# One fused Hyena and SwiGLU layer: the first joint reordered, late down-projection loads on GpSimd's queue, one operand of the last pair written down earlier

## The chip, the cores and the metric

The kernel runs on one core of one Trainium2 chip, as one program. The metric is device time in microseconds of one execution; it is given as the median of the runs, with the lowest and the highest beside it. The core has five engines with a queue each: TensorE (PE in the profile, with PEld for its weight loads), VectorE (DVE), ScalarE (ACT), GpSimd (POOL) and SyncE (SP). DMA transfers are issued here by SP (queue q1) and by POOL (queue q0), and some by ACT. Each engine carries out its queue in order; semaphores tie the queues together.

## The reference, cut to what matters

One layer on 1024 tokens of width 1024, in float32:

```python
h = rmsnorm(x, norm_mix)
z = short_conv(h @ w_in + b_in)           # 3 x 1024 columns
x0, x1, v = split(z);  s = v * x1
g = hyena_filter(...)                     # implicit long filter, 2L taps
y = irfft(rfft(s, 2L) * rfft(g, 2L))[:L]
x = x + ((y + s * skip) * x0) @ w_out + b_out
x = x + (silu(u @ w_gate) * (u @ w_up)) @ w_down,   u = rmsnorm(x, norm_ffn)
out = rmsnorm(x, norm_final)              # FFN hidden width 2816
```

## The kernel before

Every product is carried out in split float32: an operand is stored as a high part (a rounded copy, made by ACT) and a low part (what is left, a subtraction), and a product is three matmuls (`TERMS`): high by high, high by low, low by high. The low part is made in one of two ways. `split` (L128 to L130) has ACT copy the high part and DVE subtract. `low_dma` (L148 to L150) has ACT write minus the high part, and a POOL DMA that adds the source onto it in flight.

**Stages.** The input projection and the Hyena mixer run block by block up to about 410 us. The output projection follows: half 0 of its columns (`out_part`, over k = 0 to 7 of the contraction and four pairs of token blocks m), with the last block's inverse transform (`inverse_mm`) between k = 6 of pair 1 and k = 6 of pair 2; then half 1, a loop over the eight token blocks in the order `seq` = 0, 4, 1, 5, 2, 3, 6, 7 (L1310 on). This loop is the first part of the joint. Step n of it has 24 products for block j, then `turn` (eight transposes) of the block before, `x1_half` (DVE adds the residual, ACT squares, SP stores it to DRAM), `normed` (the RMS norm of the row block, in place, on DVE with a square root on ACT), and `post`, which makes the operands of the FFN from the transposed block.

**The FFN** multiplies two by two blocks in Winograd's form with seven products instead of eight. Its right operands are B11, B21, B22 and four combinations T1 to T4 of the transposed, normed blocks: `top_left` (L1091) makes the blocks of m = 0 to 3 that go into B11 and B21, with their low parts by `low_dma` for m < 3 and by DVE for m = 3; `top_sums`, with `Right`, makes T1 to T4 and B22 of blocks 4 to 7. Its left operands come from weights loaded as `wgr` and `wur`: a `Unit` is one pair of 128 hidden columns of gate or up, with a11 to a22 and four sums s[0] to s[3] (`sums`, `sum3`, `sum4`). The products of a unit are a (a11 by B11), b (a12 by B21), f, g, e (s[1], s[2], s[0] by T2, T3, T1), d (a22 by T4) and c (s[3] by B22). PSUM tiles `ab` and `dc` hold two halves each: pa and pb, pd and pc. `p1` is product a, `p1_out` copies pa away, `p2` adds product b. `w_op` (L1191) makes a left operand's two parts in one of five buffers, `OPS`, which rotate in the order in which the calls stand.

From L1306 on PE, DVE and ACT are in an order written out by hand (`manual_schedule`): first the loop, and from L1347 the rest of the joint, in which the last two blocks (6 and 7) are turned and combined while the first two units (`ug` for gate, `uu_` for up, pair 0) begin. Four weight operands there, `pre` and `pq`, are made ahead by `early_op` (L1302), which is a split by `low_dma`: `pre` holds a11 of both units, `pq` a12. POOL and SP are placed by the planner in this stage. The planner orders what isn't written by hand by a modelled timeline.

Pairs 1 to 9 (`pair`) follow, placed by the planner with SP by hand; pair 10 is `last_pair`, with PE by hand. Its results go to DRAM (`HD`), and the down projection reads them back: `product2` for p1, p5, p6, p3, p7, p2, p4, six batches each. `operands` (L1544) loads a batch's left operand on POOL (`hr`, four buffers), splits it, and splits the weights from `wds`, the down weights, which SP has loaded as quads B11, B12, B22, B21 of eleven blocks, with quarters of the residual (`load_y1`) between them. `less` forms differences of quads in place on DVE (L1614).

Of the kernel before, what the change touches and what calls it, by code (L numbers as in the profile page):

```python
# [102 lines left out]
def hyena_ffn_kernel(ctx: ExitStack, tc: tile.TileContext, a: dict, out: bass.AP):  # L103
# [904 lines left out]
    out_part(0, (6,))  # L1008
    out_part(1, (6,), (0, 1))
    inverse_mm(b)  # L1010
    out_part(1, (6,), (2,))
# [79 lines left out]
    def top_left(m, pt):  # L1091
        ms = cols_of(m)
        S.copy(u2[0][0][:, :, ms], pt)
        xt = x1[m].rearrange("p (k m) -> p k m", k=NB)
        S.copy(xt, pt)
        if m < 3:
            low_dma(u2[0][0][:, :, ms], u2[1][0][:, :, ms], xt)
            return lambda: None
        return lambda: V.tensor_tensor(
            u2[1][0][:, :, ms], pt, u2[0][0][:, :, ms].bitcast(F32), ALU.subtract  # L1100
        )
# [95 lines left out]
    class Unit:  # L1197
# [57 lines left out]
        def sums(u, eng):  # L1255
            eng.tensor_tensor(u.s[0], u.a21, u.a22, ALU.add)
            eng.tensor_tensor(u.s[1], u.s[0], u.a11, ALU.subtract)
# [40 lines left out]
    def post_late():  # L1298
        while late:
            late.pop(0)()  # L1300
# [5 lines left out]
    with tc.manual_schedule(  # L1306
# [3 lines left out]
        for n, j in enumerate(seq):  # L1310
            if n % 4 < 2:
                pts[n % 2] = mm_psum(f"po1{n}")
            hf = n // 2 % 2
            o = pts[n % 2][:, hf * 512 : (hf + 1) * 512]
            for k in range(NB):
                out_mm(o, 1, j, k)
            if n == 1:
                t_op("T1", "ab_g", ("gg0",))
                t_op("T2", "cr", ("fwd01",))
                t_op("T3", "whl1", ("hs", "wt"))  # L1320
            if 1 <= n <= 6:
                turn(seq[n - 1])
            if n == 7:
                turn(6)
                pq = slot("ss", "pq", (2, 2, 4, P), F32R)
                early_op(pq[:, 0], ug.a12)
            x1_half(j, 1, o)
            if n == 6:
                early_op(pre[:, 1], uu_.a11)
            if n < 7:  # L1330
                post_late()
                normed(j)
            if 1 <= n <= 6:
                post(seq[n - 1])
            if n == 3:
                ug = Unit(0, wg, "wg")
            if n == 4:
                uu_ = Unit(0, wu, "wu")
                pre = slot("whl0", "pre", (2, 2, 4, P), F32R)
            if n == 5:  # L1340
                early_op(pre[:, 0], ug.a11)
            if n == 6:
                post_late()
                ug.s_tag = "ab_d"
                ug.split_sum_tiles()
                ug.sums(V)
        ug.begin(True)  # L1347
        uu_.begin(True)
        r6 = Right(2, turns[6])
        r6.sums12()  # L1350
        norm_begin(7)
        r6.sum3()
        r6.high("T2")
        r6.b22_high()
        norm_end(7)
        ug.p1(pre[:, 0])
        r6.high("T3")
        r6.low("T3", None)
        early_op(pq[:, 1], uu_.a12)
        r6.low("T2", V)  # L1360
        r6.b22_low()
        ug.p1_out()
        ug.early = {"f": w_op("wg0f", ug.s[1])}
        uu_.p1(pre[:, 1])
        turn(7)
        r6.sum4()
        r6.high("T1")
        r6.low("T1", None)
        uu_.p1_out()
        r7 = Right(3, turns[7])  # L1370
        r7.sums12()
        r7.sum3()
        ug.p2(pq[:, 0])
        uu_.p2(pq[:, 1], (0, 1))
        r6.t4_high()
        r6.t4_low(None)
        r7.part("T2", V)
        r7.part("T3", V)
        ug.sum3()
        ug.early["g"] = w_op("wg0g", ug.s[2])  # L1380
# [3 lines left out]
        ug.product(ug.pb, "f", None, "T2", True, ug.early["f"])  # L1384
        V.tensor_tensor(ug.uu[:, 1], ug.uu[:, 0], ug.pb, ALU.add)
        r7.t4_high()
        r7.t4_low(None)
        r7.b22_high()
# [4 lines left out]
        ug.product(ug.pd, "e", None, "T1", True, ug.early["e"])  # L1393
        ug.sum4()
        g0 = slot("inv", "g0", (4, 512))
        ug.early["d"] = w_op("wg0d", ug.a22)
        uu_.sum_tiles()
        uu_.sums(V)
        uu_.early["f"] = w_op("wu0f", uu_.s[1])
        ug.end_products(g0[:, 1:4])  # L1400
        uu_.sum3()
        uu_.early["g"] = w_op("wu0g", uu_.s[2])
        S.activation(g0[:, 0], ug.pa, AF.Silu)
        ug.end_sums(g0[:, 1:4])
        uu_.sum4()
        uu_.product(uu_.pb, "f", None, "T2", True, uu_.early["f"])
        V.tensor_tensor(uu_.uu[:, 1], uu_.uu[:, 0], uu_.pb, ALU.add)
# [4 lines left out]
    def pair(i, ug=None, uu_=None):  # L1412
        early = ug is not None
        g = g0 if early else slot("inv", f"g{i}", (4, 512))
        if not early:
# [4 lines left out]
            ug.sums(V)  # L1420
# [5 lines left out]
        if not early:  # L1426
# [4 lines left out]
            uu_.sums(V)  # L1431
# [25 lines left out]
    def last_pair(i):  # L1457
# [6 lines left out]
        ug.sums(V)  # L1464
        uu.p1()
        uu.p1_out()
        ug.product(ug.pb, "f", ug.s[1], "T2", True)
# [7 lines left out]
        uu.sums(V)  # L1475
# [29 lines left out]
    def load_quad(x, i):  # L1505
        f, d = divmod(x, 2)
        load(wds[i][:, x], wd[i * 256 + f * P : i * 256 + (f + 1) * P, d * 512 : (d + 1) * 512])
# [4 lines left out]
    def load_y1(r, c):  # L1512
        for q in range(4):
            j, cs = 4 * r + q, slice(c * 512, (c + 1) * 512)
            load(y1[j][:, cs], X1D[j][:, cs])
# [28 lines left out]
    def operands(nm, hx, wsrc, i, n):  # L1544
# [4 lines left out]
        store(hr[:, 0:n], HD[hx][:, i : i + n, :])  # L1549
        ho = hi_lo(SETS[c][0], f"ho{nm}{i}")  # L1550
# [98 lines left out]

    bx = four(mm_psum, "bx")  # L1650
# [9 lines left out]
    V.tensor_scalar(gfin, gfin, 2.0, None, ALU.mult)  # L1660
    for i in range(NP):
        load_quad(B21, i)
    load_y1(1, 0)
# [37 lines left out]
```

## Time and profile before

| | us |
|---|---|
| median of 3 runs | 1176.32 (1175.88 to 1178.87) |
| profiled execution, time | 1177.2 |
| profiled execution, span | 1175.4 |
| PE busy | 1151.6 (98%) |
| DVE busy | 870.8 (74%) |
| ACT busy | 522.3 (44%) |
| POOL busy | 155.1 (13%) |

The profile is of one execution. The span runs from its first to its last instruction. A busy time is the sum over an engine's instructions; PE's includes work done at a lower granted clock. "L1237" is line 1237 of the kernel; an arrow reads "written tile <- read tiles", with buffer numbers left out; a bracket in a timeline row gives the engine's idle time just before it and what ended that. Times in timeline rows are microseconds from the span's start, first the start, then the length of the row, which can hold several instructions (x4).

### The profile page before, as it was taken

The page shows a single profiled execution, that of the slowest core. Times are in us where ns is not written, and L with a number is a line of the kernel's source. Part 1 is how long each engine was busy: PE and PEld are TensorE (multiplying, and loading weights), DVE is VectorE, ACT ScalarE, POOL GpSimd, SP SyncE. Part 2 cuts the span into 40 slices and gives each one's busy share as a digit, 9 for nine tenths or more (in the row PEclk, how much of TensorE's full clock was granted, in tenths as well). Part 3 has the DMA queues.
Part 4 walks back from the last instruction along what each step waited for, and adds up shares of the span by engine and source line. Part 5 has one row for each costly group of instructions (what it writes and reads, how often), then busy time and mean ns, then how long its engine had stood idle before and what let it go on. Part 6 is the DMA issues. An engine that isn't in the chain of part 4 may idle for free.

```text
span 1175.4 us, 15154 instructions
## 1 busy us (share of the span) xinstructions
PE 1151.6 (98%) x5714; PEld 970.0 (83%) x5714; DVE 870.8 (74%) x1389; ACT 522.3 (44%) x829; POOL 155.1 (13%) x218
## 2 busy tenths in 40 slices
PE   8999999999999999988999999999999999999997
PEld 6889898898988888876888888888888788788886
DVE  7688989889898895477756676666566567955675
ACT  8563553545446474365333233323333243334445
POOL 0010211112011141052001110111011110110100
PEclk9999999999999999999999999999999999999999
DMA  7456778776674799576223332324133269833323
GB/s 240 145 120 144 141 163 170 159 166 155 129 161 100 195 245 298 148 138 105 96 101 120 105 115 69 130 90 135 56 124 108 75 231 374 297 117 96 99 81 144
DMA packets 105818, 172.95 MB, mean 147 GB/s; under 512 B 7181, under 2 KB 65933, under 8 KB 105616
## 3 DMA queue, kind: packets, MB, share of 16 engines
q0 software_dynamic: 30080, 81.02, 30.5%
q1 hardware_dynamic: 75517, 90.70, 23.3%
q8 instruction: 45, 0.74, 0.2%
q10 hardware_dynamic: 146, 0.27, 0.1%
q14 instruction: 30, 0.24, 0.1%
HBM read 101.96 MB, written 40.11 MB: 121 GB/s over the span
## 4 chain that ended last, share of the span: by engine, by line
PE 85%; DVE 7%; DMA 6%; ACT 1%; issue 1%; POOL 0%; DVEq 0%; POOLq 0%; ACTq 0%; SPq 0%
PE z L140 20%; PE bx L1560 8%; PE po L914 3%; PE bz L1560 3%; PE by L1560 3%; PE pg L541 2%; PE pp L614 2%; PE pg L540 2%; DMA wd<-in_ffn_w_down_dram 2%; DMA xd<-x 1%; DMA wohl<-wo 1%; PE py L653 1%; PE py L654 1%; PE z L366 1%; PE z L693 1%; PE wu9dc L1237 1%
## 5 line engine op out<-in xcount | busy, mean ns | idle before, releaser
L140 PE MATMUL z<-uh,whl 128*128 128x512 f32 x704 | 195.4, 392 | 0.0
L140 PEld LDWEIGHTS z<-uh,whl 128*128 128x128 f32 x704 | 130.1, 188 | 25.6
L1560 PE MATMUL bx<-wop,hop 128*128 128x512 f32 x480 | 110.1, 389 | 0.8 <-DVE hop L130 0.8
L140 PE MATMUL z<-ul,whl 128*128 128x512 f32 x352 | 108.8, 390 | 0.0
L1560 PEld LDWEIGHTS bx<-wop,hop 128*128 128x128 f32 x480 | 90.0, 188 | 19.9 <-DVE hop L130 1.2
L130 DVE TENSOR_TENSOR hop<-hrp,hop 128x1024 fp32r<-128x1024 f32 (+1 forms) x40 | 45.0, 1130 | 52.3 <-ACT hop L129 52.3
L129 ACT CAST hop<-hrp 128x1024 fp32r<-128x1024 f32 (+1 forms) x40 | 38.9, 977 | 96.9 <-PE bx L1560 32.5
L140 PEld LDWEIGHTS z<-ul,whl 128*128 128x128 f32 x352 | 66.1, 188 | 14.1
L914 PE MATMUL po<-wohl,uh 128*128 128x512 f32 x256 | 75.1, 397 | 0.8 <-DMA wohl<-wo 0.7
L1030 POOL DMA_DIRECT2D hd<-g x40 | 21.6, 543 | 320.2 <-DVE g L1437 188.3
L1560 PE MATMUL by<-wop,hop 128*128 128x512 f32 x264 | 60.2, 389 | 0.0
L1560 PEld LDWEIGHTS by<-wop,hop 128*128 128x128 f32 x264 | 49.6, 188 | 10.3
L914 PEld LDWEIGHTS po<-wohl,uh 128*128 128x128 f32 x256 | 48.0, 190 | 11.3 <-DMA wohl<-wo 1.2
L194 ACT CAST whl<-wt 128x1024 fp32r<-128x1024 f32 x24 | 25.2, 1050 | 68.2 <-PE z L140 64.7
L130 DVE TENSOR_TENSOR wop<-wd,wop 128x512 fp32r<-128x512 f32 x73 | 47.7, 687 | 3.5 <-ACT wop L129 3.5
L150 POOL DMA_DIRECT2D whl<-wt x24 | 20.8, 866 | 218.9 <-ACT whl L149 131.0
L541 PE MATMUL pg<-hw,fwd 128*128 128x128 f32 x256 | 49.5, 275 | 0.0
L540 PE MATMUL pg<-hw,fwd 128*128 128x128 f32 x256 | 49.5, 275 | 0.0
L129 ACT CAST wop<-wd 128x512 fp32r<-128x512 f32 x73 | 42.2, 617 | 14.1 <-PE by L1560 4.9
L1030 POOL DMA_DIRECT2D hrp<-hd x42 | 22.3, 532 | 184.7 <-DVE hop L130 160.4
L914 PE MATMUL po<-wohl,ul 128*128 128x512 f32 x128 | 44.4, 393 | 0.0
L540 PEld LDWEIGHTS pg<-hw,fwd 128*128 128x128 f32 x256 | 39.4, 192 | 0.6
(1593 smaller groups left out, 2836.0 us busy)
## 6 DMA issues: line engine op xcount, KB each, us to landing
hrp<-hd POOLq DMA_DIRECT2D x35, 512.0 KB, 4.0
wt<-in_hy_w_in_dram SPq DMA_DIRECT2D x24, 512.0 KB, 5.0
whl<-wt POOLq DMA_DIRECT2D x24, 512.0 KB, 4.6
wgr<-in_ffn_w_gate_dram SPq DMA_DIRECT2D x22, 512.0 KB, 4.3
wur<-in_ffn_w_up_dram SPq DMA_DIRECT2D x22, 512.0 KB, 3.7
wd<-in_ffn_w_down_dram SPq DMA_DIRECT2D x44, 256.0 KB, 6.6
hd<-g POOLq DMA_DIRECT2D x40, 256.0 KB, 2.4
hd<-sx POOLq DMA_DIRECT2D x30, 256.0 KB, 2.8
```

What stands on the lines that cost most here:

```text
L129: S.copy(hi, src)
L130: (eng or V).tensor_tensor(lo, src, hi.bitcast(F32), ALU.subtract)
L140: T.matmul(pt[:, h * 512 : (h + 1) * 512], w[wi], u2[ui][h][:, k, :], start=first and ti == 0, stop=last and ti == len(TERMS) - 1,)
L150: G.dma_start(lo.bitcast(F32), src, accum_op=ALU.add)
L194: S.copy(whl[:, 0], w_raw[n])
L366: T.matmul(z_psum[n][:, lo:hi], w_hl[n][wi][:, k, :], u2[ui][lo // 512][:, k, lo % 512 : (hi - 1) % 512 + 1], start=k == 0 and ti == 0 and ...
L540: T.matmul(o, fwd[r][:, j, :], f.hw[:, j, 0, :], start=True, stop=False)
L541: T.matmul(o, fwd[2 * r][:, jj, :], f.hw[:, jj, 1, :], start=False, stop=True)
L614: T.matmul(pt[:, j * P : (j + 1) * P], fwd[r][:, j, :], z.sT[:, j, :], start=True, stop=True)
L914: T.matmul(o, u2[yi][th][:, k, m * P : (m + 1) * P], wos[h][k // 2][wi][:, k % 2, :], start=(k == 0 and ti == 0), stop=(k == NB - 1 and ti ...
L1030: G.dma_start(dst, src)
L1560: T.matmul(pt, ho[hi_][:, x, q * P : (q + 1) * P], wo_[wi][:, x, :], start=fresh and first and x == 0 and ti == 0, stop=last and x == n - ...
```

## The change: what it does

1. In half 0 of the output projection, at k = 6, the terms that need no low weight part (0 and 2) of pairs 0 and 1 come first, then term 1 of pair 0, the inverse transform, and term 1 of pair 1.
2. `top_left` makes the low part of all four blocks on DVE; three passes on ACT and three DMAs on POOL fall away. The copy into x1[m] stays.
3. In the loop, `pre` is made one step earlier (n = 4 and 5), `sum1` of `ug` stands at n = 5, `sum2` at n = 6 ahead of the norm, and the high half of the last `pq` is copied at n = 7 ahead of the square of block 7; its low half follows after `norm_begin(7)`.
4. After the loop the order of blocks 6 and 7, of the sums and of the operand splits is new: T1 of block 6 comes ahead of T3, its T4 behind the copy of block 7, the two low parts of T4 and B22 of block 7 are by DVE, and `norm_end(7)` stands behind `sums12` of block 6.
5. The order of the last products of pair 0 was d, c of gate, then f, g of up. It is now d of gate, f of up, c of gate, g of up; d stands ahead of the addition that reads pd.
6. In `last_pair`, the operand f of gate is made ahead of product a of up. PE's order stays.
7. The loads of B21 and of the quarter `load_y1(1, 0)` go from SP to POOL: they are kept in a list, and `operands` issues two of them behind its own load from its 13th call on. POOL is in the written order from p1 on.

The diff (signatures that only drop an argument are left out):

```diff
-    out_part(0, (6,))
-    out_part(1, (6,), (0, 1))
+    out_part(0, (6,), (0, 2))
+    out_part(1, (6,), (0, 2))
+    out_part(0, (6,), (1,))
     inverse_mm(b)
-    out_part(1, (6,), (2,))
+    out_part(1, (6,), (1,))
...
     def top_left(m, pt):
         ms = cols_of(m)
         S.copy(u2[0][0][:, :, ms], pt)
-        xt = x1[m].rearrange("p (k m) -> p k m", k=NB)
-        S.copy(xt, pt)
-        if m < 3:
-            low_dma(u2[0][0][:, :, ms], u2[1][0][:, :, ms], xt)
-            return lambda: None
+        S.copy(x1[m].rearrange("p (k m) -> p k m", k=NB), pt)
         return lambda: V.tensor_tensor(
             u2[1][0][:, :, ms], pt, u2[0][0][:, :, ms].bitcast(F32), ALU.subtract
         )
...
                 early_op(pq[:, 0], ug.a12)
+                S.copy(pq[:, 1, 0], uu_.a12)
             x1_half(j, 1, o)
-            if n == 6:
-                early_op(pre[:, 1], uu_.a11)
             if n < 7:
                 post_late()
+                if n == 6:
+                    ug.sum2()
                 normed(j)
...
             if n == 4:
                 uu_ = Unit(0, wu, "wu")
                 pre = slot("whl0", "pre", (2, 2, 4, P), F32R)
+                early_op(pre[:, 0], ug.a11)
             if n == 5:
-                early_op(pre[:, 0], ug.a11)
+                early_op(pre[:, 1], uu_.a11)
+                ug.s_tag = "ab_d"
+                ug.split_sum_tiles()
+                ug.sum1()
             if n == 6:
                 post_late()
-                ug.s_tag = "ab_d"
-                ug.split_sum_tiles()
-                ug.sums(V)
         ug.begin(True)
         uu_.begin(True)
+        ug.sum3()
+        norm_begin(7)
+        low_dma(pq[:, 1, 0], pq[:, 1, 1], uu_.a12)
         r6 = Right(2, turns[6])
         r6.sums12()
-        norm_begin(7)
-        r6.sum3()
+        norm_end(7)
         r6.high("T2")
         r6.b22_high()
-        norm_end(7)
+        r6.high("T1")
+        r6.low("T1", None)
         ug.p1(pre[:, 0])
+        uu_.p1(pre[:, 1])
+        r6.sum3()
+        r6.low("T2", V)
+        ug.p1_out()
+        ug.early = {"f": w_op("wg0f", ug.s[1])}
+        turn(7)
+        r6.sum4()
         r6.high("T3")
         r6.low("T3", None)
-        early_op(pq[:, 1], uu_.a12)
-        r6.low("T2", V)
         r6.b22_low()
-        ug.p1_out()
-        ug.early = {"f": w_op("wg0f", ug.s[1])}
-        uu_.p1(pre[:, 1])
-        turn(7)
-        r6.sum4()
-        r6.high("T1")
-        r6.low("T1", None)
-        uu_.p1_out()
         r7 = Right(3, turns[7])
         r7.sums12()
+        r6.t4_high()
+        r6.t4_low(None)
+        uu_.p1_out()
         r7.sum3()
         ug.p2(pq[:, 0])
         uu_.p2(pq[:, 1], (0, 1))
-        r6.t4_high()
-        r6.t4_low(None)
         r7.part("T2", V)
+        ug.early["g"] = w_op("wg0g", ug.s[2])
         r7.part("T3", V)
-        ug.sum3()
-        ug.early["g"] = w_op("wg0g", ug.s[2])
         r7.part("T1", V)
         r7.sum4()
         ug.early["e"] = w_op("wg0e", ug.s[0])
         ug.product(ug.pb, "f", None, "T2", True, ug.early["f"])
+        r7.t4_high()
+        r7.b22_high()
+        r7.t4_low(V)
         V.tensor_tensor(ug.uu[:, 1], ug.uu[:, 0], ug.pb, ALU.add)
-        r7.t4_high()
-        r7.t4_low(None)
-        r7.b22_high()
         r7.b22_low()
...
         ug.product(ug.pd, "e", None, "T1", True, ug.early["e"])
+        ug.early["d"] = w_op("wg0d", ug.a22)
         ug.sum4()
-        g0 = slot("inv", "g0", (4, 512))
-        ug.early["d"] = w_op("wg0d", ug.a22)
         uu_.sum_tiles()
-        uu_.sums(V)
+        uu_.sums()
         uu_.early["f"] = w_op("wu0f", uu_.s[1])
-        ug.end_products(g0[:, 1:4])
+        ug.early["c"] = w_op("wg0c", ug.s[3])
         uu_.sum3()
         uu_.early["g"] = w_op("wu0g", uu_.s[2])
+        g0 = slot("inv", "g0", (4, 512))
+        ug.product(ug.pc, "d", None, "T4", False, ug.early["d"])
+        V.tensor_tensor(g0[:, 3], ug.uu[:, 2], ug.pd, ALU.add)
+        uu_.product(uu_.pb, "f", None, "T2", True, uu_.early["f"])
         S.activation(g0[:, 0], ug.pa, AF.Silu)
+        uu_.sum4()
+        V.tensor_tensor(uu_.uu[:, 1], uu_.uu[:, 0], uu_.pb, ALU.add)
+        ug.product(ug.pd, "c", None, "B22", False, ug.early["c"])
         ug.end_sums(g0[:, 1:4])
-        uu_.sum4()
-        uu_.product(uu_.pb, "f", None, "T2", True, uu_.early["f"])
-        V.tensor_tensor(uu_.uu[:, 1], uu_.uu[:, 0], uu_.pb, ALU.add)
         uu_.product(uu_.pc, "g", None, "T3", True, uu_.early["g"])
...
         ug.p1_out()
-        ug.sums(V)
+        ug.sums()
+        tf = w_op(f"{ug.nm}f", ug.s[1])
         uu.p1()
         uu.p1_out()
-        ug.product(ug.pb, "f", ug.s[1], "T2", True)
+        ug.product(ug.pb, "f", None, "T2", True, tf)
...
+    behind = []
+
-    def load_quad(x, i):
+    def load_quad(x, i, put=load):
         f, d = divmod(x, 2)
-        load(wds[i][:, x], wd[...])
+        put(wds[i][:, x], wd[...])
...
         store(hr[:, 0:n], HD[hx][:, i : i + n, :])
+        for _ in range(2):
+            if behind and b >= 12:
+                behind.pop(0)()
...
+    ctx.enter_context(tc.manual_schedule(engines={mybir.EngineType.Pool}))
     bx = four(mm_psum, "bx")
...
+    def later(*x):
+        behind.append(lambda: store(*x))
+
     for i in range(NP):
-        load_quad(B21, i)
-    load_y1(1, 0)
+        load_quad(B21, i, later)
+    load_y1(1, 0, later)
```

`store` is a DMA issued by GpSimd, `load` one issued by SP.

More of the change, by code (lines that the diff above doesn't have):

```diff
@@ L1253, in p2, with sum1, sum2, sums @@
             u.product(u.pa, "b", u.a12, "B21", False, t, ks)
-        def sums(u, eng):
-            eng.tensor_tensor(u.s[0], u.a21, u.a22, ALU.add)
-            eng.tensor_tensor(u.s[1], u.s[0], u.a11, ALU.subtract)
+        def sum1(u):
+            V.tensor_tensor(u.s[0], u.a21, u.a22, ALU.add)
+        def sum2(u):
+            V.tensor_tensor(u.s[1], u.s[0], u.a11, ALU.subtract)
+        def sums(u):
+            u.sum1()
+            u.sum2()
         def sum3(u):
@@ L1430, in pair @@
             uu_.p1_out()
-            uu_.sums(V)
+            uu_.sums()
             uu_.middle()
@@ L1463, in last_pair @@
         ug.p1_out()
-        ug.sums(V)
+        ug.sums()
+        tf = w_op(f"{ug.nm}f", ug.s[1])
         uu.p1()
         uu.p1_out()
-        ug.product(ug.pb, "f", ug.s[1], "T2", True)
+        ug.product(ug.pb, "f", None, "T2", True, tf)
         V.tensor_tensor(ug.uu[:, 1], ug.uu[:, 0], ug.pb, ALU.add)
@@ L1474, in last_pair @@
         ug.product(ug.pd, "e", ug.s[0], "T1", True)
-        uu.sums(V)
+        uu.sums()
         uu.product(uu.pb, "f", uu.s[1], "T2", True)
@@ L1503, in hyena_ffn_kernel, with load_y1 @@
     B11, B12, B21, B22 = range(4)
-    def load_quad(x, i):
+    behind = []
+    def load_quad(x, i, put=load):
         f, d = divmod(x, 2)
-        load(wds[i][:, x], wd[i * 256 + f * P : i * 256 + (f + 1) * P, d * 512 : (d + 1) * 512])
+        put(wds[i][:, x], wd[i * 256 + f * P : i * 256 + (f + 1) * P, d * 512 : (d + 1) * 512])
     y1t = slot("ul1", "y1t", (4, 1024))
     y1 = [y1t[:, j] for j in range(4)]
-    def load_y1(r, c):
+    def load_y1(r, c, put=load):
         for q in range(4):
             j, cs = 4 * r + q, slice(c * 512, (c + 1) * 512)
-            load(y1[j][:, cs], X1D[j][:, cs])
+            put(y1[j][:, cs], X1D[j][:, cs])
     for i in range(NP):
```

## The prediction

> **What bounds the kernel now.** I read the page first, then the busy time by stages of 25 us, then PE's waits, then the timelines of the stages where PE has any.
>
> ```profile
> span 1175.4 us, 15154 instructions
> PE 1151.6 (98%) x5714; PEld 970.0 (83%) x5714; DVE 870.8 (74%) x1389; ACT 522.3 (44%) x829; POOL 155.1 (13%) x218
> ```
>
> PE is busy for 1151.6 of 1175.4 us, so nothing but PE's idle time and its clock can be won; 23.8 us are idle. The stages say where (columns: stage length, then busy time and count for PE, PEld, DVE, ACT and POOL; granted clock, DMA share, GB/s):
>
> ```profile
> 500.00:525.00 25.00, 22.82 (x107) 18.75 (x106) 18.47 (x40) 18.12 (x34) 14.58 (x12) 0.93 0.66 140
> 525.00:550.00 25.00, 20.44 (x88) 15.90 (x87) 18.10 (x32) 15.42 (x30) 8.93 (x7) 0.93 0.86 115
> 575.00:600.00 25.00, 25.00 (x112) 20.68 (x112) 15.72 (x23) 6.63 (x12) 3.26 (x6) 1.00 0.30 106
> 1000.00:1025.00 25.00, 24.19 (x107) 19.74 (x106) 25.00 (x40) 9.13 (x15) 2.64 (x5) 1.00 0.86 322
> ```
>
> The joint, 500 to 550 us, idles 6.7 us at a granted clock of 0.93. From 575 on the pairs fill PE. At 1000 to 1025 DVE is full and PE idles 0.8 us.
>
> ```profile
> PE wu0ab L1237 <- DMA pq<-wur: 2.6, 1, 2.6
> ...
> PE wg0ab L1237 <- DMA pre<-wgr: 1.2, 1, 1.2
> ...
> PE tp L1085 <- DVE x L1076: 0.9, 1, 0.9
> ...
> PE wg0ab L1237 <- ACT wg0u L1250: 0.8, 1, 0.8
> ```
>
> These waits (total, times, longest) and the four that rows below show in brackets all lie where the diff works. A wait costs more than its length where the clock falls behind it:
>
> ```profile
> 503.30 0.39 PE L914 MATMUL po<-wohl,ul 128*128 128x512 f32 x1
> 505.87 1.74 PE L1085 MATMUL tp<-ident,x 128*128 128x128 f32 x8 [2.18 <-issue]
> ...
> 509.52 0.39 PE L914 MATMUL po<-wohl,ul 128*128 128x512 f32 x1
> ...
> 526.55 1.04 PE L1085 MATMUL tp<-ident,x 128*128 128x128 f32 x8
> 527.34 0.47 PE L1237 MATMUL wg0ab<-uh,pre 128*128 128x512 f32 x1
> ...
> 556.13 0.47 PE L1237 MATMUL wg0dc<-uh,wg0d 128*128 128x512 f32 x1 [1.30 <-DVE g L1275]
> ```
>
> In the stage 575 to 600, 112 products fill 25.00 us with loads beside them, so one takes some 0.223 to 0.227 us start to start; eight transposes take 0.79 (526.55 to 527.34). From 503.30 to 509.52 stand six products and eight transposes, 2.2 us of work in 6.2: 4.0 are lost, 2.2 idle and 1.8 at about half speed. From 526.55 (call it X, where the output projection ends) to 556.13 stand 16 transposes and 84 products, 20.6 us of work in 29.6: 9.0 lost.
>
> **The output projection's low weights.** `out_part` at 448 us:
>
> ```profile
> 448.16 0.39 PE L914 MATMUL po<-wohl,uh 128*128 128x512 f32 x1
> 449.27 0.50 PE L914 MATMUL po<-wohl,uh 128*128 128x512 f32 x1 [0.72 <-DMA wohl<-wo]
> ```
>
> The second product needs the low weights and starts 1.11 us after the first instead of 0.23. Now eight products that don't need them come first, 1.8 us, so they have landed. No product is added, ten still stand ahead of the inverse transform. Gain **0.9 us** (0 if the inverse's own DVE work is then late, 1.0 with all of it).
>
> **Low parts on DVE (`top_left`).** Removed for m = 0, 1, 2: an ACT pass and a Pool DMA of 512 KB each. Added: a DVE subtraction, as m = 3 has today.
>
> ```profile
> 488.57 1.59 POOL L150 DMA_DIRECT2D ul<-x  x1 [22.67 <-ACT ul L149]
> 490.65 0.32 SPq L126 DMA_DIRECT2D xd<-x  x1
> 496.74 0.75 DVE L1076 SCALAR_TENSOR_TENSOR x<-x,rq,gffn 128x512 f32<-128x512 f32 x1 [3.37 <-DMA xd<-x]
> ...
> 480.87 1.42 DVE L1076 SCALAR_TENSOR_TENSOR x<-x,rq,gffn 128x512 f32<-128x512 f32 x2
> ...
> 491.41 0.16 DVE L1065 SCALAR_TENSOR_TENSOR rq<-sq 128x1 f32<-128x1 f32 x1 [0.79 <-ACT jq L1038]
> ...
> 526.36 1.22 DVE L1099 TENSOR_TENSOR ul<-tp,uh 128x1024 fp32r<-128x1024 f32 x1
> ```
>
> The Pool transfer of 488.57 goes ahead of the store of x1 at 490.65; the norm writes x1 in place and so waits 3.37 us for that store, until 496.74. DVE then carries the delay into `turn(1)` (0.9) and, through the right-half sums queued behind, into `turn(5)` (2.2 and the half clock). With the transfer gone I take the 3.37 as gone: the same two multiplications at 480.87, with no such transfer ahead, ran without a wait. Against it stands the subtraction, 1.13 us from start to start, of which 0.7 hides in the 0.79 us in which DVE waits for ACT's square just before 491.41. So the sums start at 494.4 instead of 497.4, and the first scaled half for `turn(5)` is there at 502.7. PE, no longer held at `turn(1)`, comes to it 1.1 earlier than at 503.5, at 502.4; with the second half at 503.4 the transposes end at 503.9, 0.8 late. At n = 5 and 6 DVE sets the pace: it carries the subtraction of m = 1, and the store of j = 3, behind a weight load, still takes about as long as today. I get `turn(3)` 0.9 late, `turn(6)` on time, and X at 522.7 instead of 526.55. Gain of the loop **3.8 us**, of at most 5.1 (1.1 at `turn(1)`, 4.0 at `turn(5)`); the least is nothing, since the three subtractions and the two sums that move ahead of `normed(6)` are 4.6 us of DVE work.
>
> **Weight parts earlier, and the joint's new order.**
>
> ```profile
> pre<-wgr POOLq DMA_DIRECT2D x1, 256.0 KB, 8.5
> pre<-wur POOLq DMA_DIRECT2D x1, 256.0 KB, 7.9
> ...
> pq<-wur POOLq DMA_DIRECT2D x1, 256.0 KB, 5.3
> ```
>
> ```profile
> 537.15 2.30 POOL L150 DMA_DIRECT2D pq<-wur  x1
> ...
> L1237 PE MATMUL wg0ab<-T2h,wg0f 128*128 128x512 f32 x8 | 3.7, 539 | 0.0
> ```
>
> These transfers take 5 to 8.5 us to land. `pre` moves one step of about 6 us earlier, so its 1.2 goes. The last half of `pq` was issued at 537.15, X + 10.6, and PE stood for it; its cast now precedes the loop's last square and its transfer follows the square root, about X + 4. It lands near X + 9.5, and PE asks for it at X + 11 or later: the 2.6 goes, and with it the half clock behind it, in which f's products had 539 ns instead of some 390 (about 1.7 over twelve). Product d now stands ahead of the addition that it waited for, with `uu_`'s f between d and c to cover that addition: 1.3 goes. What is late next is ACT:
>
> ```profile
> 529.53 0.63 ACT L1038 ACTIVATE jq<-x 128x512 f32<-128x512 f32 x1 [2.86 <-DVE x L1037]
> ...
> 535.83 0.57 ACT L1250 COPY wg0u<-wg0ab 128x512 f32<-128x512 f32 x1
> ...
> 538.01 0.57 ACT L1250 COPY wu0u<-wu0ab 128x512 f32<-128x512 f32 x1
> 538.48 0.59 ACT L1116 COPY tta<-tp 128x512 f32<-128x512 f32 x1
> ...
> 539.10 0.69 DVE L1117 TENSOR_TENSOR ttb<-tp,x 128x512 f32<-128x512 f32 x1 [0.85 <-ACT tta L1116]
> ```
>
> The square that was at X + 3.0 comes to X + 2.2, since DVE has fewer sums ahead of its addition. Counting ACT's and DVE's queues on in the new order with 0.55 us an ACT pass and 0.65 a DVE one: the sums of j = 6 end at X + 5.4; the norm of 7, now behind them, at X + 7.6, so `turn(7)` ends at X + 8.1 instead of 7.0; `ug.p1_out` at X + 8.3, so `ug.p2` runs to X + 11.1; and `uu_.p1_out`, behind j = 7's copy and both passes of T4, ends at X + 12.1, so `uu_.p2` waits 1.2. The T2 chain lets product f start at about X + 13.8, and 9.5 us of products follow without a wait: d starts at X + 23.4 where it was X + 29.6. Gain **6.2 us**, of at most 9.0; at worst 2, if f starts at X + 17 as today, with the 1.3 and some half clock still saved.
>
> The clock decides part of this. Waits of 1.2 and 1.3 us left it full here, the two above 2 us halved it. The Trainium skill, "TensorE: Matmul & The Clock Gate", section "What's actually happening", has the clock fall only after an idle window of about 3.4 us; no idle here was so long, so the trace doesn't agree. By the page the new waits cost only themselves up to 3.4 us; by the rows above, one that grows from 1.2 to beyond 2 costs 1.7 more.
>
> **The last pair's f.**
>
> ```profile
> 912.56 0.39 PE L1237 MATMUL wu9dc<-T1h,wu9e 128*128 128x512 f32 x1
> ...
> 915.48 0.62 ACT L129 CAST wu10a<-wur 128x512 fp32r<-128x512 f32 x1 [2.10 <-PE wu9dc L1237]
> 916.15 0.50 PE L1237 MATMUL wu10ab<-uh,wu10a 128*128 128x512 f32 x1 [0.71 <-ACT wu10a L129]
> ```
>
> Operands rotate through five buffers in the order in which they are written down. `wu10a` now has the buffer that `wu9e` leaves, at 915.3. With f created first it gets the next one, of `wu9b`, whose products end at 912.56, and f, which PE wants only at 924, waits for `wu9e`. Gain **0.8 us** (0 to 0.9; a planner that orders these anew could lose as much).
>
> **Late down loads.** Fifteen loads of 256 KB (B21 and a quarter of the residual) leave SP's end and go to Pool, two behind each operand load from the 13th on; Pool's order is fixed there.
>
> ```profile
> 1001.79 9.28 SPq L126 DMA_DIRECT2D wd<-in_ffn_w_down_dram  x11
> ...
> 1015.53 0.53 POOL L1030 DMA_DIRECT2D hrp<-hd  x1 [4.82 <-DVE hop L130]
> ```
>
> On SP nothing that matters stood behind them. Two issues of 0.53 us on Pool fit in its wait for DVE (4.8), which stays the releaser; the first product that reads B21 starts past 1107. DVE stays full at 1000 to 1025, so I leave the 0.8 there. **Nothing**, between a gain of 0.8 and a loss of as much.
>
> **The sum.** 0.9 + 3.8 + 6.2 + 0.8 = 11.7 us; I take 11, as the counted queues leave out small waits. The profiled execution took 1177.2 us, its span and 1.8 around it, and stands 0.9 above the median of 1176.32. 1177.2 - 11 = 1166.2, against the median about **1165.5**.
>
> **The rivals.** *DVE becomes the bound of the loop and the clock falls again.* For it: 4.6 us more DVE work before `turn(6)`, and the store's wait may belong partly to the 512 KB weight load issued right behind it. Then X gains nothing, the joint 3, the rest 1.7: about 1171.5. Against: that load came behind the store, the Pool transfer ahead.
>
> *The joint's chain through norm 7, `turn(7)` and T2 is as long as before*, and the change moves PE's waits to other instructions: only the 1.7 of the two small edits, lessened by new waits, 1175.
>
> *All waits close*: 0.9 + 5.1 + 9.0 + 0.8, about 1160.5. Against: ACT's queue, as counted.
>
> *Slower: the Pool loads stop DVE.* The joint's wait on L1275 shows that a write to one half of a buffer (pc) was held for a read of the other (pd). If B21's load holds the differences on the same `wd` tile likewise, those that the planner pulls ahead wait on DVE until Pool's load has landed. One such stop, with DVE already full, costs a landing of some 6.6 us, the median on the page's issue line, and 1.7 of half clock; two are 16.6 and outweigh the 11: about 1181.
>
> ```profile
> wd<-in_ffn_w_down_dram SPq DMA_DIRECT2D x44, 256.0 KB, 6.6
> ```
>
> Against: Pool runs several batches ahead of PE.
>
> **How the numbers follow.** Forecast 0.55; DVE-bound loop 0.19; chain as long as before 0.12; all waits closed 0.06; stopped DVE 0.08. The range is 1161 to 1174: it holds the forecast, the DVE-bound loop and most of the closed case, and leaves out the unchanged and slower ones. About 0.3%, 3.5 us, is what a measurement here can tell from no change. Faster 0.79 (forecast, closed, all but a little of the DVE-bound loop), same 0.13, slower 0.08.
>
> **What would show it.** Right: no store wait of more than 1 us in the norm of j = 1; `turn(5)` waiting less than 1 us at full clock; no PE wait on `pre`, `pq` or L1275; a wait of about 1 us for ACT's copy ahead of `uu_.p2`; 1.00 granted at 500 to 550. Wrong: a wait above 2 us at `turn(6)` or `turn(7)`, a new PE wait in the pairs, or DVE waiting for `wd` at L1614 after p6 begins.

## The result, and the profile after

The changed kernel takes **1164.63 us** (median of four, 1163.78 to 1164.85) beside 1176.57 of the kernel before (four runs, 1175.88 to 1178.87): 0.9896 of its time, 95% interval 0.9883 to 0.9908. The forecast was 1165.5. The profiled execution took 1164.85 us with a span of 1163.1, so the two spans differ by 12.3 us. All terms below are made against the spans.

The page of the kernel after, the span and PE's row (busy time, share, instructions):

```profile
span 1163.1 us, 15117 instructions
PE 1147.6 (99%) x5714; PEld 967.5 (83%) x5714; DVE 873.6 (75%) x1393; ACT 520.3 (45%) x825; POOL 157.3 (14%) x229
```

PE has the same 5714 instructions and 4.0 us less busy time: the stretches at half speed in the joint are gone. The other 8.3 us were idle time. The same stages as before, in the same columns (PE, PEld, DVE, ACT, POOL, granted clock, DMA share, GB/s):

```profile
500.00:525.00 25.00, 24.08 (x121) 19.41 (x120) 20.98 (x43) 16.21 (x33) 8.67 (x8) 1.00 0.51 120
525.00:550.00 25.00, 24.06 (x108) 19.18 (x107) 22.30 (x40) 16.07 (x30) 6.29 (x5) 1.00 0.68 116
```

The joint's 6.7 us of idle time at clock 0.93 are 1.9 at 1.00. In 500 to 550 PE now carries out 229 instructions, where it carried out 195. Of PE's nine waits in the part of the kernel that the diff touches three are left: 0.80 us at `turn(3)`, 0.91 for the copy of up's pa, and 1.37 at p6, which the brackets below show. Where PE stands in time is read from its timeline; first the kernel before, for a row that the prediction didn't show, then the kernel after:

```profile
483.37 1.04 PE L1085 MATMUL tp<-ident,x 128*128 128x128 f32 x8
```

```profile
482.38 1.04 PE L1086 MATMUL tp<-ident,x 128*128 128x128 f32 x8
...
501.70 1.30 PE L1086 MATMUL tp<-ident,x 128*128 128x128 f32 x8
...
515.60 1.27 PE L1086 MATMUL tp<-ident,x 128*128 128x128 f32 x8 [0.80 <-PE po L914]
...
522.19 1.03 PE L1086 MATMUL tp<-ident,x 128*128 128x128 f32 x8
...
528.55 1.28 PE L1086 MATMUL tp<-ident,x 128*128 128x128 f32 x8
...
533.78 0.50 PE L1234 MATMUL wu0ab<-uh,pq 128*128 128x512 f32 x1 [0.91 <-ACT wu0u L1247]
...
535.27 0.39 PE L1234 MATMUL wg0ab<-T2h,wg0f 128*128 128x512 f32 x1
...
544.79 0.39 PE L1234 MATMUL wg0dc<-uh,wg0d 128*128 128x512 f32 x1
...
1006.96 5.28 PE L1574 MATMUL bx<-wop,hop 128*128 128x512 f32 x22 [1.37 <-DVE hop L130]
```

The rows of eight transposes are the turns of the loop: `turn(0)` at 482.38, `turn(5)` at 501.70, `turn(3)` at 515.60, `turn(6)` at 522.19 (this is X), `turn(7)` at 528.55. So the 12.3 us split up as follows, each from the difference of two starts:

| stretch | before | after | gain |
|---|---|---|---|
| up to `turn(0)` | 483.37 | 482.38 | 0.99 |
| `turn(0)` to X | 43.18 | 39.81 | 3.37 |
| X to product d | 29.58 | 22.60 | 6.98 |
| d to the end of the span | 619.27 | 618.31 | 0.96 |

Two stalls of DVE belong to the two waits with new places; the kernel after, DVE:

```profile
491.88 1.41 DVE L1077 SCALAR_TENSOR_TENSOR x<-x,rq,gffn 128x512 f32<-128x512 f32 x2
...
512.84 0.85 DVE L1066 SCALAR_TENSOR_TENSOR rq<-sq 128x1 f32<-128x1 f32 x1 [1.11 <-ACT jq L1039]
...
1002.66 0.69 DVE L1675 TENSOR_SCALAR gfin<-gfin 128x1024 f32<-128x1024 f32 x1 [1.03 <-DMA gfin<-in_norm_final_dram]
```

The first row is the norm of block 1, which stood 3.37 us for its store and now has no wait. In the second DVE waits for ACT's square of block 3. In the third it waits for the final norm's weights.

### The profile page after: what moved, and what is told of

It reads as the page before. It is cut to its first block, busy times and chain, and to the rows that moved or that the text cites. A ratio compares the mean times of both kernels' runs of the same rounds, so it can differ in the third digit from the quotient of the medians.

```text
span 1163.1 us, 15117 instructions
## 1 busy us (share of the span) xinstructions
PE 1147.6 (99%) x5714; PEld 967.5 (83%) x5714; DVE 873.6 (75%) x1393; ACT 520.3 (45%) x825; POOL 157.3 (14%) x229
## 4 chain that ended last, share of the span: by engine, by line
PE 85%; DVE 8%; DMA 3%; ACT 1%; issue 1%; SPq 1%; POOL 0%; DVEq 0%; POOLq 0%; ACTq 0%
PE z L140 20%; PE bx L1574 7%; PE po L914 3%; DMA wd<-in_ffn_w_down_dram 3%; PE bz L1574 3%; PE by L1574 3%; PE pg L541 2%; PE pp L614 2%; PE pg L540 2%; PE py L653 1%; PE py L654 1%; PE z L366 1%; PE z L693 1%; PE wu4dc L1234 1%; PE wu9dc L1234 1%
```

## The experiments

Each is one edit of the kernel after or of the kernel before. None changes what is computed.

**The low parts of the first three blocks by DMA again**, in the kernel after:

```diff
-        S.copy(x1[m].rearrange("p (k m) -> p k m", k=NB), pt)
+        xt = x1[m].rearrange("p (k m) -> p k m", k=NB)
+        S.copy(xt, pt)
+        if m < 3:
+            low_dma(u2[0][0][:, :, ms], u2[1][0][:, :, ms], xt)
+            return lambda: None
```

> The changed kernel, with the low parts of blocks 0 to 2 again by an ACT pass and a Pool transfer; all else stays changed. Theory A (the Pool transfer ahead of the store makes the norm wait): the second multiplication of the norm of block 1 waits 3 us or more for its store again, turn(5) waits about 2 us and the clock falls behind it, and the loop ends some 3.5 us later than in the changed kernel: about 1168. Theory B (the store is late for the weight load behind it, and the loop gained by the sums and weight parts that moved): no wait of more than 1 us comes back, and the time stays within 1 us of 1164.6.

Measured: 1168.14 us (1167.03 to 1168.77), ratio to the kernel before 0.9927 (0.9912 to 0.9941); the span is 1167.0, 3.9 more than after. This kernel's DVE, then its PE:

```profile
495.82 0.75 DVE L1077 SCALAR_TENSOR_TENSOR x<-x,rq,gffn 128x512 f32<-128x512 f32 x1 [3.37 <-DMA xd<-x]
```

```profile
504.94 1.27 PE L1086 MATMUL tp<-ident,x 128*128 128x128 f32 x8 [2.20 <-issue]
511.55 1.03 PE L1086 MATMUL tp<-ident,x 128*128 128x128 f32 x8
...
525.29 1.03 PE L1086 MATMUL tp<-ident,x 128*128 128x128 f32 x8
...
547.59 0.39 PE L1238 MATMUL wg0dc<-uh,wg0d 128*128 128x512 f32 x1
```

The store's wait is back to the hundredth, and `turn(5)` waits 2.20 us again. X is 3.1 later than after; d follows at X + 22.3, so the joint behind it loses nothing. But the clock didn't fall: the eight transposes take 1.27 us (1.74 in the kernel before, behind 2.18 us), and the next turn follows 6.61 us later (8.00 in the kernel before). So the wait is caused as the prediction said; the half clock behind it does not always come.

**Only block 0's low part on DVE**, in the kernel before:

```diff
-        if m < 3:
+        if 0 < m < 3:
```

> The kernel before, with the low part of block 0 alone by DVE, blocks 1 and 2 by the Pool transfer as before. Theory A: the 3.37 us wait of the norm of block 1 falls below 0.5, PE's wait at turn(1) is gone and that at turn(5) below 1 us at full clock, while the waits of blocks 3 and 6 for their stores stay near 1 us; about 4.5 us less than before. Theory B: 3 us or more remain, and the time stays that of before within 1 us.

One run: 1171.53 us, 5.0 less than the kernel before, where 4.5 was expected. DVE's norm of block 1, then PE:

```profile
492.66 1.42 DVE L1076 SCALAR_TENSOR_TENSOR x<-x,rq,gffn 128x512 f32<-128x512 f32 x2
```

```profile
502.49 1.27 PE L1085 MATMUL tp<-ident,x 128*128 128x128 f32 x8
...
517.25 0.66 PE L1085 MATMUL tp<-ident,x 128*128 128x128 f32 x4 [1.14 <-DVE x L1076]
...
523.23 1.03 PE L1085 MATMUL tp<-ident,x 128*128 128x128 f32 x8
...
537.99 0.73 PE L1237 MATMUL wu0ab<-uh,pq 128*128 128x512 f32 x2 [1.48 <-DMA pq<-wur]
```

The norm no longer waits for its store, and `turn(5)` has no wait. One transfer of three, the one issued 2 us ahead of the store, held this whole stretch, and X comes 3.3 us earlier than before. `turn(3)` still waits 1.14 us for a norm that waits for its store; with all low parts on DVE (next run) it doesn't. Behind X, PE still waits 1.26 us for `pre`, but only 1.48 for `pq`, at full clock; d starts at 550.96, 27.73 us after X where the kernel before took 29.58. And SP's queue in this kernel has the same loads of 512 KB right behind the store as before, so these don't hold it:

```profile
490.44 0.32 SPq L126 DMA_DIRECT2D xd<-x  x1
490.85 6.98 SPq L126 DMA_DIRECT2D wgr<-in_ffn_w_gate_dram  x2
```

**All low parts on DVE and nothing else**, in the kernel before: `top_left` as in the diff.

> The kernel before with the low parts of blocks 0 to 2 on DVE and nothing else changed. Theory A (the loop's gain is this edit's): the store wait of block 1 is gone, turn(1) and turn(5) cost below 1 us together at full clock, and the waits at the joint (pre, pq, L1275) stay; some 4 us less than before, 1172.5 to 1173.5. Theory B (the three subtractions make DVE the bound of the loop, and only the moved sums and weight parts made room for them): turn(3) or turn(6) wait above 1.5 us and the loop gains below 2 us.

One run: 1169.65 us, span 1167.7, 7.7 less than before. PE:

```profile
482.79 1.04 PE L1085 MATMUL tp<-ident,x 128*128 128x128 f32 x8
...
521.92 1.03 PE L1085 MATMUL tp<-ident,x 128*128 128x128 f32 x8
...
535.75 0.73 PE L1233 MATMUL wu0ab<-uh,pq 128*128 128x512 f32 x2 [1.55 <-DMA pq<-wur]
...
548.68 0.47 PE L1233 MATMUL wg0dc<-uh,wg0d 128*128 128x512 f32 x1 [1.76 <-DVE g L1271]
```

`turn(0)` to X takes 39.13 us, 4.05 less than before and 0.7 less than in the whole change, and no turn of the loop waits. The rest is outside the loop: X to d is 26.76, 2.8 less than before, though the joint's order is the old one. The expectation had the joint's waits unchanged and so a time 3 us higher. The first `pre` no longer queues behind a 512 KB transfer: it lands after 4.3 us, not 8.5, and its wait of 1.20 is gone without its being made earlier. The wait for `pq` is 1.55 and not 2.57, without a half clock behind it. That second part doesn't need all three transfers gone: with block 0 alone on DVE, `pre` still landed after 8.5 us and PE waited 1.26 us for it, but 1.9 of the 2.8 was there already, at `pq`. In that run `pq` was issued at X + 9.9 and landed after 4.8 us, in the kernel before at X + 10.6 and after 5.3; what made it earlier is not separated. So this one edit is worth 6.9 us alone (4.05 and 2.8, one run), but only 3.9 as the last of all: the two meet in the waits on `pre` and `pq`.

**The last half of `pq` at its old place**, in the kernel after:

```diff
-                S.copy(pq[:, 1, 0], uu_.a12)
...
-        low_dma(pq[:, 1, 0], pq[:, 1, 1], uu_.a12)
...
         r6.low("T3", None)
+        early_op(pq[:, 1], uu_.a12)
```

> The changed kernel with both parts of up's a12 made where they were before, behind the low part of T3 of block 6. Theory A (only the place of the transfer made PE wait): it is issued some 6 us later, lands near 537 to 539, and PE, which wants it at 534, waits 3 us or more, with the clock at half behind it if the wait is beyond 2 us; 4 to 6 us slower. Theory B (the new order of the sums frees Pool and DMA, so it lands sooner): a wait below 1.5 us.

One run: 1171.38 us, span 1169.6. PE:

```profile
534.23 0.50 PE L1234 MATMUL wu0ab<-uh,pq 128*128 128x512 f32 x1 [2.08 <-ACT wu0u L1247]
...
537.57 1.22 PE L1234 MATMUL wu0ab<-uh,pq 128*128 128x512 f32 x2 [2.61 <-DMA pq<-wur]
...
539.45 0.63 PE L1234 MATMUL wg0ab<-T2h,wg0f 128*128 128x512 f32 x1
...
549.65 0.39 PE L1234 MATMUL wg0dc<-uh,wg0d 128*128 128x512 f32 x1
```

The wait for the transfer is back at 2.61 us, with products at 0.63 us behind it, and d starts 4.9 us later than after. The cast and the pass on ACT, which now stand ahead of the copy of pa, make that copy later too (2.08 for 0.91).

**Product d behind the addition that reads pd**, in the kernel after:

```diff
-        ug.product(ug.pc, "d", None, "T4", False, ug.early["d"])
         V.tensor_tensor(g0[:, 3], ...)
+        ug.product(ug.pc, "d", None, "T4", False, ug.early["d"])
```

> The changed kernel with gate's product d behind the addition that reads pd, as before. Theory A (the write to pc is held for the read of pd, which share a tile): PE waits about 1.3 us at d again, 1.5 us slower. Theory B (d was late for its operands, which now are early): no wait.

One run: 1177.52 us. PE, then DVE:

```profile
549.92 0.77 PE L1234 MATMUL wg0dc<-uh,wg0d 128*128 128x512 f32 x1 [4.97 <-DVE g L1408]
...
550.91 1.06 PE L1234 MATMUL wg0dc<-uh,wg0d 128*128 128x512 f32 x2
...
555.11 0.39 PE L1234 MATMUL wu0ab<-T2h,wu0f 128*128 128x512 f32 x1
```

```profile
544.88 0.69 DVE L130 TENSOR_TENSOR wu0f<-wu0s,wu0f 128x512 fp32r<-128x512 f32 x1 [0.74 <-ACT wu0f L129]
...
549.10 0.68 DVE L1408 TENSOR_TENSOR g<-wg0u,wg0dc 128x512 f32<-128x512 f32 x1
```

The hold is as described: d, which writes pc, waits for an addition that only reads pd, in the same tile. Its size is not 1.3 but 4.97 us, since in the new order seven subtractions and sums stand on DVE from 544.88 on ahead of the addition, while PE was done with e at 544.95 (549.92 less 4.97). The clock halves behind it (two products 1.06 us, 0.62 in the kernel after), and f of up starts 7.6 us later than after. The rest of this run's 12.7 us is not the joint's: p6 waits 2.2 and 0.9 us for DVE, and the stage from 1000 to 1025 has a granted clock of 0.86, which is some 3.5 us of full speed. Whether the edit caused that is not shown.

**`turn(7)` held back**: in the kernel after, the sum s[2] of gate repeated k times ahead of `norm_end(7)`; it writes the same values.

```diff
+        for _ in range(5):
+            ug.sum3()
         norm_end(7)
```

> The changed kernel with one sum (sum3 of gate, the same value each time) carried out five times more on DVE ahead of the norm of block 7, 3.0 us, so that PE waits about 3 us at turn(7). Theory A (a wait beyond 2 us halves the clock for about 3.5 us): transposes and products behind it at half speed, 1.7 us lost on top: 4.5 to 5 us slower. Theory B (only an idle stretch of about 3.4 us does, and where the stretch falls matters): full speed behind it, 3 us slower.

> The changed kernel with the sum repeated three times, 1.8 us, ahead of the norm of block 7. Theory A (a wait of 2 us or more halves the clock): a wait of 2.1 to 2.2 us at turn(7) and half speed behind it, 1.6 us on top, of which the 0.9 wait for the copy of up's product a absorbs a part. Theory B (such a wait halves the clock only where it falls right in a window that runs by itself): full speed behind it, and PE later by the 2.1 less what the 0.9 absorbs.

Five times, one run: 1168.57 us, span 1166.8. Three times, one run: 1167.75 us, span 1166.0. PE with five, then with three:

```profile
531.88 1.30 PE L1086 MATMUL tp<-ident,x 128*128 128x128 f32 x8 [3.35 <-issue]
...
533.84 1.05 PE L1234 MATMUL wg0ab<-uh,pq 128*128 128x512 f32 x2
...
538.71 0.39 PE L1234 MATMUL wg0ab<-T2h,wg0f 128*128 128x512 f32 x1
```

```profile
530.71 1.27 PE L1086 MATMUL tp<-ident,x 128*128 128x128 f32 x8 [1.90 <-issue]
...
537.02 0.40 PE L1234 MATMUL wg0ab<-T2h,wg0f 128*128 128x512 f32 x1
```

Behind 3.35 us the clock halves, behind 1.90 it stays. With three repeats f is 1.75 us later, about the wait. With five it is 3.44 later, hardly more than the wait itself, since the slow products ran for the most part in the time in which PE would have waited for the copy: that wait of 0.91 is gone in this run. So the chain through norm 7 and `turn(7)` does carry the joint, with next to no slack: what DVE does longer ahead of it comes out at f.

**f of the last pair made late again**, in the kernel after:

```diff
-        tf = w_op(f"{ug.nm}f", ug.s[1])
...
-        ug.product(ug.pb, "f", None, "T2", True, tf)
+        ug.product(ug.pb, "f", ug.s[1], "T2", True)
```

> The changed kernel, with the gate operand f of the last pair written down behind product a of up again. Theory A (the rotation of five buffers decides): wu10a gets the buffer of wu9e again and PE waits about 0.7 us for its copy; 0.9 us slower, 1165.5. Theory B (the planner's new order of the pairs removed the wait): no wait, within 0.3 us of 1164.6.

Measured: 1165.87 us (1164.85 to 1166.37), ratio 0.9907 (0.9893 to 0.9922). PE:

```profile
904.44 0.50 PE L1234 MATMUL wu10ab<-uh,wu10a 128*128 128x512 f32 x1 [0.71 <-ACT wu10a L129]
```

The wait of the kernel before is back at the same 0.71 us. The span is not longer (1163.0); p6 waits only 0.62 us in this run. The medians, 1.2 apart, can't be told apart with these intervals.

**The late loads on SP again**, with POOL placed by the planner again, in the kernel after:

```diff
-    ctx.enter_context(tc.manual_schedule(engines={mybir.EngineType.Pool}))
...
-        load_quad(B21, i, later)
-    load_y1(1, 0, later)
+        load_quad(B21, i)
+    load_y1(1, 0)
```

> The changed kernel, with the fifteen late loads back at the end of SP's queue and Pool placed by the planner. Theory A (nothing waits for them on either queue): within 0.8 us of 1164.6, and PE's wait at the start of p6 stays, since DVE is full there. Theory B (on Pool they take transfer time from the operand loads, and so p6 waits 1.37 us instead of 0.81): p6's wait falls back to 0.8 and the time by 0.6. Theory C (the moved loads are worth something): 1 us or more slower, and DVE waits for the down weights of p5 and p6 grow.

Measured: 1165.0 us (1163.65 to 1166.37), ratio 0.99 (0.9881 to 0.9919): no difference from the change. p6 waits 1.24 us here too, in its second batch; another 0.32 us stands at p1, at 956.62.

**Three of the waits that are left**, in the kernel after: the first `pre` is made a step later, behind the norm of block 3; the copy of up's pa stands ahead of T4's two passes; the doubling of `gfin` is written behind p5.

```diff
                 normed(j)
+            if n == 5:
+                early_op(pre[:, 0], ug.a11)
...
             if n == 4:
...
-                early_op(pre[:, 0], ug.a11)
...
+        uu_.p1_out()
         r6.t4_high()
         r6.t4_low(None)
-        uu_.p1_out()
...
-    V.tensor_scalar(gfin, gfin, 2.0, None, ALU.mult)
...
     product2("p5", ...)
+    V.tensor_scalar(gfin, gfin, 2.0, None, ALU.mult)
```

> The changed kernel with three more moves: the cast of the first weight part (pre of gate) stands behind the norm of block 3 instead of ahead of its square on ACT; the copy of up's product a stands ahead of both passes of T4 on ACT; and the scaling of the final gain on DVE stands behind p5. Theory A (the three waits that are left, 0.8 at turn(6), 0.9 for the copy, 1.4 at p6, come from those queue positions): turn(6)'s wait falls below 0.3 and the copy's to nothing, p6's at least by half; some 2 us less, 1162.5. Theory B (DVE sets the pace of the loop and of p6): the waits stay or move to the next instruction, within 0.5 us of 1164.6.

Measured: 1164.07 us (1163.64 to 1165.89), ratio 0.9899 (0.9886 to 0.9913), span 1161.9. PE:

```profile
514.83 1.27 PE L1086 MATMUL tp<-ident,x 128*128 128x128 f32 x8
...
543.67 0.39 PE L1234 MATMUL wg0dc<-uh,wg0d 128*128 128x512 f32 x1
```

`turn(3)` (the expectation calls it `turn(6)`) doesn't wait and starts 0.77 us earlier; of the three edits only the first stands ahead of it. The copy's wait is gone, with 0.23 left for T2's low part. d starts 1.1 us earlier than after. p6 still waits 1.30: DVE still has the doubling ahead of p6's operands, at 1001.43 behind a wait of 0.96 for its load, though it is written behind p5.

**The differences of p7 on POOL**, on top of the three edits just shown:

```diff
-    product2("p7", bx, 6, less(B11, B12, B11), False, ...)
+    product2("p7", bx, 6, less(B11, B12, B11, G), False, ...)
```

> The kernel with the three further moves, and the eleven weight differences of p7 on Pool instead of DVE. Theory A (p6 waits because the planner puts p7's differences on a full DVE ahead of p6's operands): DVE between 975 and 1015 us has some 7 us less to do, PE's wait at p6 (1.3) falls below 0.3, 1.4 us faster, about 1162.7. Theory B (p6 waits for the landing of its operands, or the planner fills the room with other work): the wait stays above 0.8. Theory C: Pool, in written order, is held by the differences and its operand loads come late, 2 us or more slower.

Measured: 1165.82 us (1164.79 to 1167.24), ratio 0.9908 (0.9892 to 0.9925), span 1164.2. DVE:

```profile
1002.87 0.69 DVE L1684 TENSOR_SCALAR gfin<-gfin 128x1024 f32<-128x1024 f32 x1 [6.48 <-DMA gfin<-in_norm_final_dram]
```

PE at p6, and the stage around it (columns as above):

```profile
1005.96 31.36 PE L1575 MATMUL bx<-wop,hop 128*128 128x512 f32 x130 [1.24 <-DVE hop L130]
```

```profile
1000.00:1025.00 25.00, 23.35 (x95) 18.60 (x94) 15.54 (x21) 9.50 (x14) 6.39 (x12) 0.93 0.58 195
```

DVE now has time to spare, stands 6.48 us for the load of `gfin` with p6's operands queued behind it, and p6 waits 1.24 and 0.42 us all the same. A full DVE was not the cause here; what came into view is the doubling that waits for its load. The clock also falls here, to 0.93 over the stage, which is some 1.75 us, though neither wait is long; that is most of the 2.3 us by which this span exceeds that of the three edits alone (1161.9).

**The load of `gfin` ahead of B22's**, in the kernel after alone:

```diff
+    gfin = slot("vz", "gfin")
+    load(gfin, a["norm_final"].partition_broadcast(P))
     for i in range(NP):
         load_quad(B22, i)
...
-    gfin = slot("vz", "gfin")
-    load(gfin, a["norm_final"].partition_broadcast(P))
```

> The kernel after with one edit: the load of the final norm's weights (gfin, 512 KB on SP) stands ahead of the loads of B22, not behind them. Nothing of the computation is left out. What is open: p6's first product waits 1.37 us for DVE in the kernel after, where the kernel before had 0.81, while the doubling of gfin stood 1.03 us on DVE for its load with the operand subtractions of p6 behind it; with the differences of p7 taken off DVE that stand grew to 6.48 and p6 still waited 1.24 and 0.42. Theory A, the stand for gfin is the cause: the load now lands some 10 us or more ahead of its use, DVE doesn't stand for it, and p6 waits about 0.3 us (1.37 less 1.03), at most 0.6; the span falls by about 1. Theory B, the order of the subtractions among the differences of p7 is the cause: DVE doesn't stand either, but p6 waits 1 us or more, as in the run with the loads on SP, where gfin was there in time and p6 waited 1.24 and 0.4.

Measured: 1163.98 us (1163.31 to 1164.82), ratio 0.9888 (0.9872 to 0.9905), span 1162.4. PE:

```profile
1006.20 5.96 PE L1574 MATMUL bx<-wop,hop 128*128 128x512 f32 x25 [0.50 <-DVE hop L130]
```

DVE doubles `gfin` 18 us earlier, at 984.6, without a wait, and p6 waits 0.50 us where it waited 1.37. That is the size that the stand of 1.03 explains, so theory A holds here, with one reserve: the planner also set some of the differences in another order, and with the loads on SP p6 waited 1.24 us, in its second batch, while DVE doubled `gfin` at 1001.15 without a wait. (The 0.4 that the expectation adds there is the 0.32 at p1.) The stand for `gfin` is one cause of p6's wait, the order of the differences, by that run, a second.

The two kernels that close waits have the lowest medians, 1163.98 and 1164.07, but neither can be told from the change's 1164.63. The two together were not run.

## Why the prediction was right, step by step

**The output projection's low weights**, 0.9 predicted: 0.99, and the wait is gone. It was not undone by itself. In the run with the low parts alone, which keeps the old order here, the wait was only 0.2 us and `turn(0)` stood at 482.79, so the gain is 0.4 to 1.0, by the execution it is held against. That it is a gain is clear: all eleven kernels with the new order come to `turn(0)` between 482.17 and 482.58, the three with the old one between 482.79 and 483.37.

**The low parts on DVE**, 3.8 for the loop: 3.37. The mechanism is right, both ways: the transfer ahead of the store brought back gives the same 3.37 us stall, and taking away that one transfer of three ends it. `turn(1)` and `turn(5)` wait no more, so the rival in which DVE becomes the bound has fallen. `turn(3)` is 0.8 late where 0.9 was predicted, but the reason given was wrong: not DVE's subtraction and block 3's store, but ACT. `pre` moved one step earlier puts a cast and a pass of ACT ahead of block 3's square, which DVE then awaits for 1.11 us; with `pre` a step later the wait is gone, and with the low parts alone it never arises. The prediction took the earlier `pre` for a gain and didn't count ACT's queue for it. It is no gain even on PE's side: with the low parts alone, and with `pre` a step later, PE has no wait on `pre` either.

**The joint**, 6.2: 6.98. The counted queues came out well: f at X + 13.1 (13.8 predicted), `turn(7)` ending at X + 7.6 (8.1), the copy's wait 0.91 us (1.2), no wait on `pre`, `pq` or the addition, clock 1.00. That the time of X to d is a chain, and which one, is shown by holding `turn(7)`. What the sum had wrong is how it is split: the price of d's order was put at 1.3, the wait that it had in the old order. In the new one, the wait would be 4.97 us and the half clock as well, so this order is no small edit but what keeps the rest of the gain. And 2.8 of the joint's gain come with the low parts already: 1.2 because `pre` no longer queues behind a transfer of 512 KB, the rest for the most part at `pq`, for a cause that stays open. The prediction had all that the low parts gain in the loop.

**The last pair's f**, 0.8: 0.87. In the kernel before, e of up starts at 912.56 and `wu10a` at 916.15, 3.59 us later; the kernel after takes 2.72, without a wait:

```profile
901.14 0.39 PE L1234 MATMUL wu9dc<-T1h,wu9e 128*128 128x512 f32 x1
...
903.86 0.39 PE L1234 MATMUL wu10ab<-uh,wu10a 128*128 128x512 f32 x1
```

That the place of f causes it is shown by the wait that came back; in the time of the whole kernel it couldn't be told. **The late loads**, nothing: nothing, in 1165.0 beside 1164.63. The rival in which POOL's loads stop DVE is not seen; the kernel after, DVE, its longest wait for those tiles:

```profile
975.88 0.69 DVE L1628 TENSOR_TENSOR wd<-wd 128x512 f32<-128x512 f32 x1 [1.25 <-DMA wd<-in_ffn_w_down_dram]
```

A wait of 1.27 for such a tile was there ahead of p6 in the kernel before too, and PE has none at that time. **p6's wait**, left at 0.81, became 1.37: DVE stands 1.03 us for `gfin` right ahead of p6's operands (in the kernel before the wait stood in p6's second batch, now in its first). So the 0.96 from d to the end are 0.87 at f, 0.56 lost at p6, and 0.46 behind the last store of the output, which ACT issues at 1171.19 in the kernel before and at 1159.35 after, 4.2 and 3.8 us ahead of the end of the span. No engine computes there, and the change doesn't touch it. The 0.2 left are not followed further.

**The sum**: 11.7 with 11 taken; 12.3 in the spans, 11.9 in the medians. The four terms came to 12.2. That they stay so near 11.7 is in part luck, as the loop gave 0.4 less than its term and the joint 0.8 more. Of the 0.7 kept back for small waits 0.56 was spent at p6; the waits of 0.80 and 0.91 were in the terms already. And the rival in which the POOL loads stop DVE comes to about 1182 by its own sum (1176.3 - 11 + 16.6), not 1181; nothing hangs on it.

**The clock** was treated as a threshold near 2 us. As a warning that is borne out, as a rule it isn't. In the loop and the joint it fell behind 2.18, 2.57, 3.35 and 4.97 us, and behind 2.61 that followed on 2.08; it stayed full behind 1.90 and less, and behind 2.20. At p6 not even that holds. There 2.21 us left it full with three repeats ahead of `turn(7)`, and also with the last half of `pq` late, where 0.39 stood just ahead; with d behind the addition it fell behind 0.88 and 2.21, and with p7's differences on POOL 0.42 and 1.24 us were enough.

## What to carry to other kernels

An addition in flight by DMA looks free, since no compute engine carries it; look at what stands behind it on the DMA engines. Here one of 512 KB ahead of a store of 256 KB held an in-place norm for 3.37 us, and a DVE subtraction of 1.13 us in its place paid for itself several times: in the loop, and again in the 1.2 us for which PE had waited for a transfer queued behind another such addition.

When a step is made earlier to cover a transfer, count it on every queue that it passes: the earlier `pre` opened a wait of 0.8 us through ACT, and the one of 1.2 that it was to close had another cause. And price a hold (d behind the addition) by what stands on the releasing engine in the new order, not by the wait it shows in the old one.

## What the runs showed of the hardware

The time from issue to landing of one transfer depended here on what was ahead of it. The kernel after, its DMA issues (size, median us from issue to landing):

```profile
pre<-wgr POOLq DMA_DIRECT2D x1, 256.0 KB, 4.2
pre<-wur POOLq DMA_DIRECT2D x1, 256.0 KB, 4.3
```

The same two transfers for `pre` landed after 8.5 and 7.9 us in the kernel before, with the 512 KB ones on the queue; the prediction had taken 5 to 8.5 us for fixed. The run with the low parts back on DMA has both in one kernel: gate's `pre`, issued 3.4 us ahead of a 512 KB transfer, landed after 4.2 us, and up's, issued 1.2 us behind it, after 7.5.

The half clock is not a matter of the wait's length alone: a wait of 2.18 us halved it, one of 2.20 us at the same place of the same loop did not, and with p7's differences on POOL it fell at p6 behind 0.42 and 1.24 us. The Trainium skill, "TensorE: Matmul & The Clock Gate", section "What's actually happening", describes a free-running window, by which the phase would count as well as the length. The pair 2.18 and 2.20 agrees with that, but no run varies the phase alone; the idle window of about 3.4 us that the page gives for the fall does not agree with a fall after 2.18, nor with that at p6.
